# Rotary embedding on one core: units of 4 MiB with 32 KB rows, and a small sine table spread over the partitions by TensorE

## The chip, the cores and the metric

The kernel runs on one core of a Trainium2 chip. The metric is the time of one execution in microseconds (us) as the device reports it. A profile's span is shorter than the time: it goes from the first to the last recorded instruction. In the listings SP, ACT, POOL, DVE and PE are SyncE, ScalarE, GpSimd, VectorE and TensorE, and PEld is TensorE's weight load. A cast load is a load that turns fp32 into fp16 on the way. A DMA "lands" when its end is reported. Slices of the span and units are counted from 0.

## The reference

```python
# x: (8, 8, 1024, 64) float32, freqs: 32, positions: 0..1023, scale 0.5
angles = np.outer(positions * scale, freqs)          # 1024 x 32
cos, sin = np.cos(angles), np.sin(angles)
x_first, x_second = x[..., :32], x[..., 32:]
out_first  = x_first * cos - x_second * sin
out_second = x_first * sin + x_second * cos
```

16.8 MB come in and 16.8 MB go out. The table of sines and cosines is the same for all 64 pairs of batch and head.

## The kernel before

It cuts x into 8 units of 8 heads. (In the cuts of the two kernels here, `...` stands for what is left out; in those of the change the calls of `pin`, which keep an instruction in program order, are left out too.) A unit is 128 partitions x 4096 fp32, so one partition's row is 16 KB of contiguous HBM. Each partition holds 64 positions, and 16 partitions hold a head.

```python
X0f = xin.tile([P, N], FP32, name="X0f")                 # unit 0 in two fp32 halves, from SP and ACT
nc.sync.dma_start(out=X0f[:, : N // 2], in_=xv[0][:, : N // 2])
...                                                      # positions, freqs, second half: ACT's queue
def load(u):                                             # units 1..7: cast to fp16 on the way, POOL's queue
    nc.gpsimd.dma_start(out=X[u].rearrange("p k h j -> p (k h j)"), in_=xv[u])
...                                                      # cfreq = scale/2pi * freqs on all partitions; posf: positions
y = tmp.tile([P, K, half], FP32)                         # 128 x 64 x 32: the whole table, on every partition
nc.vector.tensor_tensor(out=y, in0=posf..., in1=cfreq..., op=ALU.mult)
...                                                      # m, r: range reduction; then sin, ra, cos
for i, u in enumerate((1, 2, 0, *range(3, NU))):
    ps = prods.tile([P, K, 2, half], FP16, tag="ps")     # two buffers
    nc.vector.tensor_tensor(out=ps, in0=X[u], in1=sin_b, op=ALU.mult)
    nc.vector.tensor_tensor(out=X[u], in0=X[u], in1=cos_b, op=ALU.mult)
    nc.vector.tensor_tensor(out=X[u][:, :, 0, :], in0=X[u][:, :, 0, :], in1=ps[:, :, 1, :], op=ALU.subtract)
    nc.vector.tensor_tensor(out=X[u][:, :, 1, :], in0=ps[:, :, 0, :], in1=X[u][:, :, 1, :], op=ALU.add)
    OUT = xout.tile([P, N], FP32, tag="O")
    nc.scalar.copy(out=OUT, in_=X[u]...)                 # back to fp32
    (nc.gpsimd if i < NU // 2 else nc.sync).dma_start(out=ov[u], in_=OUT)
```

## Time and profile before

| What | Before | Where from |
|---|---|---|
| time | 84.59 us median (84.48 to 84.63) | 6 runs |
| span | 82.6 to 83.8 us, median 82.8; the profiled one 83.1 | 44 runs beside the experiments, and the profile |
| VectorE busy | 62.5 us (75%) | the page |
| DMA | full from 2 to 81 us, 405 GB/s of HBM traffic over the span | the page's slices; 33.56 MB / 82.8 us |

The profiled execution of the kernel before was one of the slower ones, by 0.3 us. A comparison of the two profiles alone would be wrong by that much.

### The profile page before, as it was taken

The page shows a single profiled execution, that of the slowest core. Times are in us where ns is not written, and L with a number is a line of the kernel's source. Part 1 is how long each engine was busy: PE and PEld are TensorE (multiplying, and loading weights), DVE is VectorE, ACT ScalarE, POOL GpSimd, SP SyncE. Part 2 cuts the span into 40 slices and gives each one's busy share as a digit, 9 for nine tenths or more (in the row PEclk, how much of TensorE's full clock was granted, in tenths as well). Part 3 has the DMA queues.
Part 4 walks back from the last instruction along what each step waited for, and adds up shares of the span by engine and source line. Part 5 has one row for each costly group of instructions (what it writes and reads, how often), then busy time and mean ns, then how long its engine had stood idle before and what let it go on. Part 6 is the DMA issues. An engine that isn't in the chain of part 4 may idle for free.

```text
span 83.1 us, 154 instructions
## 1 busy us (share of the span) xinstructions
PE 1.1 (1%) x4; PEld 0.9 (1%) x4; DVE 62.5 (75%) x40; ACT 37.4 (45%) x12; POOL 6.7 (8%) x17
## 2 busy tenths in 40 slices
PE   0014000000000000000000000000000000000000
PEld 0013000000000000000000000000000000000000
DVE  0005999699999999999999999999999999000000
ACT  0600005999295098059129408805912950880000
POOL 4970000000002000200200200000000000000000
DMA  2799999999999999999999999999999999999990
GB/s 51 248 363 280 280 272 249 213 225 213 205 217 213 229 209 213 213 209 229 162 379 410 442 418 442 434 434 426 418 457 418 434 442 418 434 418 450 426 426 8
DMA packets 2482, 26.22 MB, mean 316 GB/s; under 512 B 290, under 2 KB 306, under 8 KB 306
## 3 DMA queue, kind: packets, MB, share of 16 engines
q0 software_dynamic: 1584, 15.73, 66.4%
q1 hardware_dynamic: 720, 9.44, 27.4%
q10 hardware_dynamic: 178, 1.06, 3.2%
HBM read 16.79 MB, written 16.78 MB: 404 GB/s over the span
## 4 chain that ended last, share of the span: by engine, by line
DVE 72%; ACT 7%; DMA 6%; DVEq 1%; PE 1%; issue 1%; ACTq 1%
DVE X L137 22%; DVE ps L136 21%; DVE X L138 12%; DVE X L141 10%; DMA freq_row<-in_freqs_dram 6%; ACT OUT L145 4%; DVE r L117 3%; DVE y L108 3%; ACT sinT L121 2%; DVE m L115 1%; DVEq L177 1%; PE cfreq L93 1%; PE pos_ps L101 1%; ACTq L66 0%; DVE posf L105 0%
## 5 line engine op out<-in xcount | busy, mean ns | idle before, releaser
L145 ACT CAST OUT<-X 128x4096 f32<-128x4096 f16 x8 | 28.8, 3605 | 25.0 <-DVE X L141 25.0
L136 DVE TENSOR_TENSOR ps<-X,sinT 128x4096 f16<-128x4096 f16 x8 | 18.3, 2284 | 0.7 <-ACT sinT L121 0.7
L137 DVE TENSOR_TENSOR X<-X,cosT 128x4096 f16<-128x4096 f16 x8 | 18.3, 2292 | 0.3
L138 DVE TENSOR_TENSOR X<-X,ps 128x2048 f16<-128x2048 f16 x8 | 9.8, 1225 | 0.3
L141 DVE TENSOR_TENSOR X<-ps,X 128x2048 f16<-128x2048 f16 x8 | 9.7, 1217 | 0.0
L121 ACT ACTIVATE sinT<-r 128x2048 f16<-128x2048 f32 x1 | 1.9, 1910 | 9.9 <-DVE r L117 9.9
L146 POOL DMA_DIRECT2D out_dram<-OUT x4 | 2.1, 534 | 39.7 <-ACT OUT L145 39.7
L74 POOL DMA_DIRECT2D X<-in_x_dram x7 | 3.9, 569 | 0.8 <-POOLq L163 0.8
L128 ACT CAST X<-X0f 128x4096 f16<-128x4096 f32 x1 | 3.6, 3589 | 0.0
L96 DVE CAST pos_row<-pos_i 16x64 f32<-16x64 int32 x1 | 0.2, 182 | 3.1 <-DMA pos_i<-in_positions_dram 3.1
L105 DVE COPY posf<-pos_ps 128x64 f32<-128x64 f32 x1 | 0.2, 224 | 2.8 <-PE pos_ps L101 2.8
L117 DVE SCALAR_TENSOR_TENSOR r<-m,y 128x2048 f32<-128x2048 f32 x1 | 2.3, 2293 | 0.0
L108 DVE TENSOR_TENSOR y<-posf,cfreq 128x2048 f32<-128x2048 f32 x1 | 2.3, 2286 | 0.0
L121 ACT ACT_TABLE_LOAD x1 | 1.3, 1283 | 2.1 <-issue 2.1
L127 ACT ACTIVATE cosT<-ra,quarter 128x2048 f16<-128x2048 f32 x1 | 2.0, 1987 | 0.0
L115 DVE TENSOR_SCALAR m<-y 128x2048 f32<-128x2048 f32 x1 | 1.2, 1226 | 0.0
L123 DVE TENSOR_SCALAR ra<-r 128x2048 int32<-128x2048 int32 x1 | 1.2, 1226 | 0.0
L89 DVE MEMSET coef<- 1x128 f32 x1 | 0.2, 165 | 0.8 <-PEq L163 0.8
L93 PE MATMUL cfreq<-freq_row,coef 1*128 1x32 f32 x2 | 0.6, 392 | 6.0 <-DMA freq_row<-in_freqs_dram 6.0
L101 PE MATMUL pos_ps<-pos_row,sel 16*128 16x64 f32 x2 | 0.7, 433 | 0.0
L93 PEld LDWEIGHTS cfreq<-freq_row,coef 1*128 1x128 f32 x2 | 0.5, 305 | 6.0 <-issue 6.0
L101 PEld LDWEIGHTS pos_ps<-pos_row,sel 16*128 16x128 f32 x2 | 0.5, 328 | 0.0
(7 smaller groups left out, 1.0 us busy)
## 6 DMA issues: line engine op xcount, KB each, us to landing
out_dram<-OUT POOLq DMA_DIRECT2D x4, 2048.0 KB, 20.5
out_dram<-OUT SPq DMA_DIRECT2D x4, 2048.0 KB, 10.8
X<-in_x_dram POOLq DMA_DIRECT2D x7, 1024.0 KB, 24.4
X0f<-in_x_dram SPq DMA_DIRECT2D x1, 1024.0 KB, 5.2
X0f<-in_x_dram ACTq DMA_DIRECT2D x1, 1024.0 KB, 11.8
pos_i<-in_positions_dram ACTq DMA_DIRECT2D x1, 8.0 KB, 3.4
freq_row<-in_freqs_dram ACTq DMA_DIRECT2D x1, 0.1 KB
```

The lines of the kernel that those rows point to most:

```text
L74: nc.gpsimd.dma_start(out=X[u].rearrange("p k h j -> p (k h j)"), in_=xv[u])
L101: nc.tensor.matmul(out=pos_ps, lhsT=sel.rearrange("q a b -> q (a b)"), rhs=pos_row, start=True, stop=True)
L108: pin(nc.vector.tensor_tensor(out=y, in0=posf.unsqueeze(2).broadcast_to((P, K, half)), in1=cfreq.unsqueeze(1).broadcast_to((P, K, half)), ...
L117: pin(nc.vector.scalar_tensor_tensor(out=r, in0=m, scalar=_MAGIC, in1=y, op0=ALU.subtract, op1=ALU.subtract))
L121: pin(nc.scalar.activation(out=sinT, in_=r, func=AF.Sin, bias=0.0, scale=-_TWO_PI_DN))
L128: pin(nc.scalar.copy(out=X[0].rearrange("p k h j -> p (k h j)"), in_=X0f))
L136: pin(nc.vector.tensor_tensor(out=ps, in0=X[u], in1=sin_b, op=ALU.mult))
L137: pin(nc.vector.tensor_tensor(out=X[u], in0=X[u], in1=cos_b, op=ALU.mult))
L138: pin(nc.vector.tensor_tensor(out=X[u][:, :, 0, :], in0=X[u][:, :, 0, :], in1=ps[:, :, 1, :], op=ALU.subtract))
L141: pin(nc.vector.tensor_tensor(out=X[u][:, :, 1, :], in0=ps[:, :, 0, :], in1=X[u][:, :, 1, :], op=ALU.add))
L145: pin(nc.scalar.copy(out=OUT, in_=X[u].rearrange("p k h j -> p (k h j)")))
L146: (nc.gpsimd if i < NU // 2 else nc.sync).dma_start(out=ov[u], in_=OUT)
```

## The change

Two things. First, units of 16 heads (4 MiB) with 32 KB rows for three of the four cast loads and for the first two stores. This saves row overhead. Second, each position's sine and cosine are computed once, 8 positions a partition. Sixteen matmuls with selection matrices of zeros and ones spread them over the partitions, and sixteen copies bring them out of PSUM, the memory into which TensorE writes. The matrices (`sel`) are made on GpSimd by a memset and a select by index (`affine_select`), called "the select" below. This shortens the start of VectorE.

```diff
-    HEADS = 8
+    HEADS = 16
...
-    pos_i64 = consts.tile([HP, K], positions.dtype)            # 16 rows of 512 B
+    pos_i64 = consts.tile([P, K8], positions.dtype)            # 128 rows of 64 B
...
-    sel = consts.tile([HP, HEADS, HP], FP32)
+    sel = consts.tile([P, G, HEADS, HP], FP16)                 # 128 x 2048
+    nc.gpsimd.dma_start(out=Xf[0][:, :NH], in_=xv[0][:, :NH])  # half of unit 0, cast
     nc.gpsimd.memset(sel, 0.0)
+    nc.gpsimd.dma_start(out=Xf[1], in_=xv[1])
     nc.gpsimd.affine_select(...)
+    for u in range(2, NU):
+        nc.gpsimd.dma_start(out=Xf[u], in_=xv[u])
...
-    y = tmp.tile([P, K, half], FP32)                           # 2048 columns
+    y = tmp.tile([P, K8, half], FP32)                          # 256 columns; m, r, ra, sin, cos too
...
+    for g in range(G):                                         # 16
+        ps = spread.tile([P, 2, K8, half], FP32, tag="g")
+        nc.tensor.matmul(out=ps, lhsT=sel[:, g], rhs=tab, start=True, stop=True)
+        dst = T[:, :, g * K8 : (g + 1) * K8, :]
+        if g % 2 == 0 and g < G // 2:
+            nc.vector.tensor_copy(out=dst, in_=ps)
+        else:
+            nc.scalar.copy(out=dst, in_=ps)
...
+    for u in range(NU):                                        # 4 units, two halves each
+        for s in range(2):
+            pr = tmp.tile([P, KH, 2, half], FP16, tag="pr")    # one buffer
+            ...                                                # the same four operations, then the ACT copy
+            if u >= NU // 2:
+                nc.sync.dma_start(out=ov[u][:, ns], in_=OUT[:, ns])
+        if u < NU // 2:
+            nc.gpsimd.dma_start(out=ov[u], in_=OUT)            # 4 MiB
```

More of the change, by code (lines that the diff above doesn't have):

```diff
@@ L18 @@
 _TWO_PI_DN = float(np.float32(np.uint32(0x40C90FDA).view(np.float32)))
-BUF_O = 4
-BUF_P = 2
 @with_exitstack
@@ L34 @@
     nc = tc.nc
+    pin = tc.keep_in_program_order
     B, Hh, S, D = x.shape
@@ L44 @@
     NU = NBH // HEADS
-    assert S % HP == 0 and D == 2 * half and NBH % HEADS == 0
+    KH = K // 2
+    NH = KH * D
+    K8 = S // P
+    G = P // HP
+    W = K8 * half
+    assert S % HP == 0 and D == 2 * half and NBH % HEADS == 0 and G * K8 == K
     fscale = float(scale)
@@ L54 @@
     psum = ctx.enter_context(tc.tile_pool(name="psum", bufs=1, space=bass.MemoryType.PSUM))
+    spread = ctx.enter_context(tc.tile_pool(name="spread", bufs=6, space=bass.MemoryType.PSUM))
     xin = ctx.enter_context(tc.tile_pool(name="xin", bufs=1))
-    xout = ctx.enter_context(tc.tile_pool(name="xout", bufs=BUF_O))
-    prods = ctx.enter_context(tc.tile_pool(name="prods", bufs=BUF_P))
-    X0f = xin.tile([P, N], FP32, name="X0f")
-    pin = tc.keep_in_program_order
-    nc.sync.dma_start(out=X0f[:, : N // 2], in_=xv[0][:, : N // 2])
-    pos_i64 = consts.tile([HP, K], positions.dtype)
-    pin(nc.scalar.dma_start(out=pos_i64, in_=positions.rearrange("(q k) -> q k", k=K)))
+    xout = ctx.enter_context(tc.tile_pool(name="xout", bufs=3))
+    X0f = xout.tile([P, N], FP32, tag="O")
+    Q = NH // 2
+    pin(nc.sync.dma_start(out=X0f[:, :Q], in_=xv[0][:, NH : NH + Q]))
+    pos_i64 = consts.tile([P, K8], positions.dtype)
+    pin(nc.scalar.dma_start(out=pos_i64, in_=positions.rearrange("(p k) -> p k", k=K8)))
     freq_row = consts.tile([1, half], FP32)
     pin(nc.scalar.dma_start(out=freq_row, in_=freqs[None, :]))
-    pin(nc.scalar.dma_start(out=X0f[:, N // 2 :], in_=xv[0][:, N // 2 :]))
+    pin(nc.scalar.dma_start(out=X0f[:, Q:NH], in_=xv[0][:, NH + Q :]))
     X = [xin.tile([P, K, 2, half], FP16, name=f"X{u}") for u in range(NU)]
-    def load(u):
-        nc.gpsimd.dma_start(out=X[u].rearrange("p k h j -> p (k h j)"), in_=xv[u])
-    sel = consts.tile([HP, HEADS, HP], FP32)
-    load(1)
-    nc.gpsimd.memset(sel, 0.0)
-    nc.gpsimd.affine_select(
+    Xf = [t.rearrange("p k h j -> p (k h j)") for t in X]
+    sel = consts.tile([P, G, HEADS, HP], FP16)
+    pin(nc.gpsimd.dma_start(out=Xf[0][:, :NH], in_=xv[0][:, :NH]))
+    pin(nc.gpsimd.memset(sel, 0.0))
+    pin(nc.gpsimd.dma_start(out=Xf[1], in_=xv[1]))
+    pin(nc.gpsimd.affine_select(
         out=sel, in_=sel, compare_op=ALU.not_equal, fill=1.0, base=0,
-        pattern=[[0, HEADS], [-1, HP]], channel_multiplier=1,
-    )
+        pattern=[[-1, G], [0, HEADS], [-G, HP]], channel_multiplier=1,
+    ))
     for u in range(2, NU):
-        load(u)
+        pin(nc.gpsimd.dma_start(out=Xf[u], in_=xv[u]))
     coef = consts.tile([1, P], FP32)
@@ L93 @@
     nc.tensor.matmul(out=cfreq, lhsT=coef, rhs=freq_row, start=True, stop=True)
-    pos_row = consts.tile([HP, K], FP32)
+    posf = consts.tile([P, K8], FP32)
     pin(nc.vector.tensor_copy(
-        out=pos_row,
-        in_=pos_i64.bitcast(I32).rearrange("p (k t) -> p k t", t=2)[:, :, 0],
-    ))
-    pos_ps = psum.tile([P, K], FP32)
-    nc.tensor.matmul(
-        out=pos_ps, lhsT=sel.rearrange("q a b -> q (a b)"), rhs=pos_row, start=True, stop=True
-    )
-    posf = consts.tile([P, K], FP32)
-    pin(nc.vector.tensor_copy(out=posf, in_=pos_ps))
-    y = tmp.tile([P, K, half], FP32)
+        out=posf, in_=pos_i64.bitcast(I32).rearrange("p (k t) -> p k t", t=2)[:, :, 0]
+    ))
+    y = tmp.tile([P, K8, half], FP32)
     pin(nc.vector.tensor_tensor(
         out=y,
-        in0=posf.unsqueeze(2).broadcast_to((P, K, half)),
-        in1=cfreq.unsqueeze(1).broadcast_to((P, K, half)),
+        in0=posf.unsqueeze(2).broadcast_to((P, K8, half)),
+        in1=cfreq.unsqueeze(1).broadcast_to((P, K8, half)),
         op=ALU.mult,
     ))
-    m = tmp.tile([P, K, half], FP32)
+    m = tmp.tile([P, K8, half], FP32)
     pin(nc.vector.tensor_scalar(out=m, in0=y, scalar1=_MAGIC, scalar2=None, op0=ALU.add))
-    r = tmp.tile([P, K, half], FP32)
+    r = tmp.tile([P, K8, half], FP32)
     pin(nc.vector.scalar_tensor_tensor(
@@ L119 @@
     ))
-    sinT = consts.tile([P, K, half], FP16)
-    pin(nc.scalar.activation(out=sinT, in_=r, func=AF.Sin, bias=0.0, scale=-_TWO_PI_DN))
-    ra = tmp.tile([P, K, half], FP32)
+    tab = consts.tile([P, 2, K8, half], FP16)
+    pin(nc.scalar.activation(out=tab[:, 0], in_=r, func=AF.Sin, bias=0.0, scale=-_TWO_PI_DN))
+    ra = tmp.tile([P, K8, half], FP32)
     pin(nc.vector.tensor_scalar(
@@ L125 @@
     ))
-    cosT = consts.tile([P, K, half], FP16)
-    pin(nc.scalar.activation(out=cosT, in_=ra, func=AF.Sin, bias=quarter, scale=-_TWO_PI_DN))
-    pin(nc.scalar.copy(out=X[0].rearrange("p k h j -> p (k h j)"), in_=X0f))
-    cos_b = cosT.unsqueeze(2).broadcast_to((P, K, 2, half))
-    sin_b = sinT.unsqueeze(2).broadcast_to((P, K, 2, half))
-    for i, u in enumerate((1, 2, 0, *range(3, NU))):
-        ps = prods.tile([P, K, 2, half], FP16, tag="ps")
-        pin(nc.vector.tensor_tensor(out=ps, in0=X[u], in1=sin_b, op=ALU.mult))
-        pin(nc.vector.tensor_tensor(out=X[u], in0=X[u], in1=cos_b, op=ALU.mult))
-        pin(nc.vector.tensor_tensor(
-            out=X[u][:, :, 0, :], in0=X[u][:, :, 0, :], in1=ps[:, :, 1, :], op=ALU.subtract
-        ))
-        pin(nc.vector.tensor_tensor(
-            out=X[u][:, :, 1, :], in0=ps[:, :, 0, :], in1=X[u][:, :, 1, :], op=ALU.add
-        ))
-        OUT = xout.tile([P, N], FP32, tag="O")
-        pin(nc.scalar.copy(out=OUT, in_=X[u].rearrange("p k h j -> p (k h j)")))
-        (nc.gpsimd if i < NU // 2 else nc.sync).dma_start(out=ov[u], in_=OUT)
+    pin(nc.scalar.activation(out=tab[:, 1], in_=ra, func=AF.Sin, bias=quarter, scale=-_TWO_PI_DN))
@@ new lines @@
+    T = consts.tile([P, 2, K, half], FP16)
+    for g in range(G):
+        ps = spread.tile([P, 2, K8, half], FP32, tag="g")
+        nc.tensor.matmul(
+            out=ps.rearrange("p t k j -> p (t k j)"),
+            lhsT=sel[:, g].rearrange("s h q -> s (h q)"),
+            rhs=tab.rearrange("s t k j -> s (t k j)"),
+            start=True, stop=True,
+        )
+        dst = T[:, :, g * K8 : (g + 1) * K8, :]
+        if g % 2 == 0 and g < G // 2:
+            pin(nc.vector.tensor_copy(out=dst, in_=ps))
+        else:
+            pin(nc.scalar.copy(out=dst, in_=ps))
@@ new lines @@
+    pin(nc.scalar.copy(out=Xf[0][:, NH:], in_=X0f[:, :NH]))
+    for u in range(NU):
+        OUT = xout.tile([P, N], FP32, tag="O")
+        for s in range(2):
+            ks = slice(s * KH, (s + 1) * KH)
+            ns = slice(s * NH, (s + 1) * NH)
+            Xs = X[u][:, ks]
+            sin_b = T[:, 0, ks].unsqueeze(2).broadcast_to((P, KH, 2, half))
+            cos_b = T[:, 1, ks].unsqueeze(2).broadcast_to((P, KH, 2, half))
+            pr = tmp.tile([P, KH, 2, half], FP16, tag="pr")
+            pin(nc.vector.tensor_tensor(out=pr, in0=Xs, in1=sin_b, op=ALU.mult))
+            pin(nc.vector.tensor_tensor(out=Xs, in0=Xs, in1=cos_b, op=ALU.mult))
+            pin(nc.vector.tensor_tensor(
+                out=Xs[:, :, 0, :], in0=Xs[:, :, 0, :], in1=pr[:, :, 1, :], op=ALU.subtract
+            ))
+            pin(nc.vector.tensor_tensor(
+                out=Xs[:, :, 1, :], in0=pr[:, :, 0, :], in1=Xs[:, :, 1, :], op=ALU.add
+            ))
+            pin(nc.scalar.copy(out=OUT[:, ns], in_=Xf[u][:, ns]))
+            if u >= NU // 2:
+                pin(nc.sync.dma_start(out=ov[u][:, ns], in_=OUT[:, ns]))
+        if u < NU // 2:
+            pin(nc.gpsimd.dma_start(out=ov[u], in_=OUT))
```

## The prediction

> **What bounds the kernel now.** I began with the slices of the page, because a kernel that only streams 16.8 MB in and 16.8 MB out should first be asked whether its DMA engines ever rest.
>
> ```profile
> DVE  0005999699999999999999999999999999000000
> ACT  0600005999295098059129408805912950880000
> ...
> DMA  2799999999999999999999999999999999999990
> GB/s 51 248 363 280 280 272 249 213 225 213 205 217 213 229 209 213 213 209 229 162 379 410 442 418 442 434 434 426 418 457 418 434 442 418 434 418 450 426 426 8
> ```
>
> One slice is 83.1/40 = 2.08 us. The DMA row is full from slice 2 to slice 38; VectorE starts in slice 3 and ends in slice 33. The GB/s row halves in the load phase only because a load that casts fp32 to fp16 is counted by the bytes that it writes: 213 written is 426 read from HBM. So the rate is nearly flat.
>
> The chain that ended last says something else, and I don't follow it to the end:
>
> ```profile
> DVE 72%; ACT 7%; DMA 6%; DVEq 1%; PE 1%; issue 1%; ACTq 1%
> ```
>
> It goes back through VectorE because its last compute piece is the ACT cast that starts at 70.86 us and takes 3.60. That ends at 74.46; the span ends at 83.1. One 2 MiB store cannot explain 8.6 us if the queues are empty, so I looked at the stores' landings and at the DMA by window:
>
> ```profile
> L146 SPq DMA_DIRECT2D out_dram<-OUT x4: 332/332/343, 53.7 to 74.5; - x4
> ...
> DMA to landing us min/median/max: 7.7/16.1/21.9
> ```
>
> ```profile
> 0.00:4.00 4.00, 0.00 (x0) 0.00 (x0) 0.17 (x2) 1.28 (x1) 2.86 (x10) 1.00 0.52 147
> 4.00:8.00 4.00, 1.08 (x4) 0.92 (x4) 1.01 (x3) 0.00 (x0) 1.68 (x4) 1.00 1.05 324
> 18.00:36.00 18.00, 0.00 (x0) 0.00 (x0) 17.83 (x11) 9.81 (x3) 1.07 (x2) 1.00 1.04 217
> ...
> 46.00:78.00 32.00, 0.00 (x0) 0.00 (x0) 24.54 (x15) 15.15 (x5) 0.53 (x1) 1.00 1.01 432
> ```
>
> The last two columns are the DMA share and GB/s. In 18 to 36 us the engines read 2 x 217 = 434 GB/s, in 46 to 78 us they write 432. The quickest store landed 7.7 us after its issue, though 2.1 MB at 432 GB/s is 4.9 us: each store stands in a line. The kernel is bound by DMA from about 2 us to about 82 us. VectorE and ScalarE come second, but not by much: if the queues were empty, the last store, issued at 74.5, would need some 1.3 us to start (my allowance; SP's first load is issued at 0.75 us and the DMA row stirs just short of 2) and 4.9 to move, ending at 80.7. The compute side has about 1 us of slack.
>
> **What the Trainium skill says.** "DMA: Bandwidth & Descriptors", section "Where 436 GB/s comes from", gives 16 x 32 B x 850 MHz = 435.2 GB/s as the ceiling of the SBUF ports. The trace agrees: 432 and 434 are within 1% of it. The same page, "Queues, rings and completion order", says that an engine takes turns between queues packet by packet, and "Issuing engines are not separate DMA queues" says that using several issuing engines saves only issue time. The trace agrees as far as it shows it: SP's and POOL's stores together move 432 GB/s in 46 to 78 us, no more than one direction did before. "TensorE: Matmul & The Clock Gate", section "Wait — 56ns, not 53.3ns?", gives 426.7 ns between matmuls of 512 columns in a cold array, 215.7 warm; the trace of before has no such matmul.
>
> **The change, part by part.**
>
> *Longer rows.* Before, 14 of the 16 MiB of loads go in cast loads of 2 MiB, with rows of 16 KB in HBM, and all 16 MiB of stores too. After, 12 MiB of cast loads (3 units) and 8 MiB of stores (2 units) have rows of 32 KB: 20 of 32 MiB. The rest stays: 2 MiB fp32 loads with 8 KB rows, one 2 MiB cast load, four half-unit stores. The number of bytes is the same. What can a longer row save? Only the cost per row. From the window 46 to 78:
>
> ```profile
> DMA packets 955, 13.81 MB, mean 432 GB/s; under 512 B 112, under 2 KB 112, under 8 KB 112
> ...
> q1 hardware_dynamic: 481, 7.09, 51.8%
> q0 software_dynamic: 474, 6.72, 49.0%
> ```
>
> The shares sum to 100.8% of 16 engines: 516 us of packet time for 843 rows of 16 KB (13.81 MB / 16384), 612 ns each. At the skill's 435.2 GB/s (27.2 B/ns an engine) a row takes 602 ns. So some 10 ns a row are overhead, and the 100.8% says that rows overlap a little and hide part of it. By rate the total loss is (435.2 - 432)/435.2, 0.7% of the 77.7 us that 33.55 MB take at 432 GB/s, or 0.57 us. Half of that goes away on 20 of 32 MiB: 0.57 x 0.5 x 0.63 = 0.18 us. Even if the overhead per row were twice what I read, it would be under 0.4 us.
>
> *Positions as 128 rows of 64 B instead of 16 of 512 B.* Eight small packets an engine in place of one. I put them at 25 to 30 ns each (an estimate from nothing but the overhead of a row above and a little for the access), so up to 0.2 us of DMA time, at the worst moment, the start. It also delays the positions and the frequencies behind them in the same queue: they may land up to 2 us later than now (now freqs' landing at 5.9 us starts the table).
>
> *The table built small.* y, r (2.29 us each), m and ra (1.23) on 2048 columns become four operations on 256. Taking (2286 - 224)/(2048 - 64) = 1.04 ns per column from y and posf gives about 0.16 + 256 x 1.04 = 0.43 us for y and r, and 0.3 for m. sin and cos (1.91, 1.99) become about 0.4 and 0.5. Removed from the path: pos_ps and posf (0.7), and 9.7 - 2.0 = about 7 us from positions to cos. Added: 16 matmuls 128x512 with a weight load each, at 0.45 us, cold; 12 casts on ACT, at 192 + 512 x 0.833 = 0.62 us each (fixed part and slope from the 3605 ns cast of 4096 columns and the 1910 ns sine of 2048), and 4 on VectorE at 0.16 + 512 x 1.04 = 0.7. The first half of the table (8 tiles) paces at TensorE's 0.45: 3.6 us plus the last copy, 0.7. With freqs landed at 6 to 7.5 us the small table is done at 8.6 to 10, the first half of the spread at 13 to 14.5. VectorE now starts at 15.24. It needs the first half of unit 0 too, which shares the engines with the two fp32 loads (4 MiB together), and lands about where unit 1 lands now, 13.4 us (12.1 after its issue at 1.3). So VectorE starts at 13.5 to 14.5, 1 to 2 us earlier.
>
> *The eight half-units.* Same operations and shapes: 2.29 + 2.29 + 1.22 + 1.22, 6.92 us from one to the next as now, so VectorE ends at about 69 to 70 and the last ACT cast at 72.5 to 74. ACT must finish 12 copies (until about 16.5) and the cast of unit 0's second half (3.6) before the second half-unit at 20.4: just in time, a wait of up to 1 us possible. All this only gives the compute side slack of 2 to 3 us instead of 1. On the path that sets the end it is worth nothing.
>
> *Supply of stores.* Loads end at about 42 us, as now (slice 19 to 20). Unit 0 is stored whole at about 31 us, unit 1 at 45, then halves at 52, 59, 66 and 73. At 432 GB/s from 42 us the engines have written 8.6 MB at 62 us (ready by then: 12.6) and 13.2 at 72.5 (ready 14.7): no gap. Units twice as large in the POOL stores do not starve the queue because loads cover the first 42 us.
>
> Sum: -0.2 (rows) + 0.1 (small packets), -0.1 us: 84.5 becomes 84.4.
>
> **Rivals.** (1) *The table was on the path, and the time falls by its 1 to 2 us or more*: for it, the chain, 72% VectorE; against it, DMA rows full to slice 38 and landings of 7.7 us and more. It would give 82.5 to 83.5. (2) *The row overhead is larger than it looks, above all for casts*: the window 18 to 36 has a share of 104%, rows of about 627 ns. If those 25 ns over 602 all vanished by half on the 20 MiB, 80 rows of 16 KB an engine would save 80 x 12 = 1.0 us: 83.5. Against it: the rate there is 434, so the rows overlap. (3) *The compute side takes over*: GpSimd has to fill and select 128x2048 instead of 16x128 (select now 0.33 us), the positions come late, the copies are slow. VectorE would have to start later than about 16.5 us to show; then 85 to 86. (4) *A gap at the start*, unit 1's load behind the larger memset: 4 MiB are queued before it, about 9.8 us of work, so no.
>
> **Range and chances.** Both states are DMA-bound with the same bytes at 99% of the ceiling, so little can move. The 80% range is 83.6 to 85.1, its low end from rival 2, its high end from a worse start. Faster by over 2% needs 82.8: 5%. Slower by over 2% needs 86.2: 3%.
>
> **What would show it.** DMA full from slice 2 to 38 again, 430 to 434 GB/s in both phases, half as many packets in q0; ACT's last cast ending 1 to 2 us earlier, the last store's landing time longer by as much. I am wrong if the rate in a phase moves by over 1%, if the DMA row has a hole, or if the first full slice of DMA shifts.

## The result

The changed kernel takes 84.88 us (84.82 to 85.06, 6 runs) against 84.59 of before. The ratio is 1.0041, interval 1.0028 to 1.0055. That is above noise a little slower. Executions over 1.5% slower than the fastest of the same kernel are left out of the means. A ratio is the mean time of one kernel's fast runs over that of the other's fast runs of the same rounds, so it is not quite the ratio of the medians.

The slices of the changed kernel's page, to be laid beside those of before:

```profile
DVE  0029657999899999999999999999999999400000
ACT  0600337999993098059219607903940880492000
...
DMA  3899997997998899799989989998999999999991
GB/s 51 327 319 269 301 341 170 254 254 151 230 254 190 190 254 238 158 238 254 127 349 412 507 364 428 475 460 357 420 436 412 428 444 412 452 420 436 436 412 55
...
q0 software_dynamic: 864, 15.73, 66.3%
```

DMA again stays full from slice 2 to slice 38. Both rows jump more, but this is only the grain of the view: a row of 32 KB is booked whole in the slice where it starts. With each record spread over its time, the engines are busy for 98% or more of each slice from 1 to 38. Queue q0 moves the same 15.73 MB in 864 packets instead of 1584. Slice 1 has 327 GB/s against 248: the start is better. (This row counts cast loads by what they write; a count by what is read from HBM, under e5 and e9, has 1.50 MB against 1.35 by 6 us.)

The windows and the landings, as before (the last two columns are DMA share and GB/s):

```profile
0.00:4.00 4.00, 0.00 (x0) 0.00 (x0) 0.17 (x2) 1.28 (x1) 2.95 (x7) 1.00 0.56 181
...
18.00:36.00 18.00, 0.00 (x0) 0.00 (x0) 17.40 (x11) 11.09 (x5) 0.54 (x1) 0.57 1.02 218
36.00:44.00 8.00, 0.00 (x0) 0.00 (x0) 7.86 (x6) 4.44 (x2) 0.00 (x0) 0.50 1.04 262
46.00:78.00 32.00, 0.00 (x0) 0.00 (x0) 24.98 (x15) 15.19 (x5) 0.53 (x1) 0.50 1.00 430
```

```profile
DMA to landing us min/median/max: 6.8/12.3/19.7
```

Steady rates are those of before within the grain of the view. The quickest store lands 6.8 us after its issue instead of 7.7. So the last store waits less, which means the compute side is nearer to being the bound, not further from it. The groups and the order of time say why:

```profile
L98 DVE CAST posf<-pos_i 128x8 f32<-128x8 int32 x1 | 2.5, 2496 | 4.7 <-DMA pos_i<-in_positions_dram 4.7
L82 POOL TENSOR_SCALAR_AFFINE_SELECT sel<-sel 128x2048 f16<-128x2048 f16 x1 | 3.9, 3865 | 0.1
```

```profile
4.29 3.87 POOL L82 TENSOR_SCALAR_AFFINE_SELECT sel<-sel 128x2048 f16<-128x2048 f16 x1
5.69 2.50 DVE L98 CAST posf<-pos_i 128x8 f32<-128x8 int32 x1 [4.69 <-DMA pos_i<-in_positions_dram]
...
14.61 2.29 DVE L149 TENSOR_TENSOR pr<-X,T 128x4096 f16<-128x4096 f16 x1 [0.31 <-ACT T L136]
...
22.02 2.29 DVE L149 TENSOR_TENSOR pr<-X,T 128x4096 f16<-128x4096 f16 x1 [0.40 <-ACT X L137]
...
27.82 1.22 DVE L154 TENSOR_TENSOR X<-pr,X 128x2048 f16<-128x2048 f16 x1
29.07 2.29 DVE L149 TENSOR_TENSOR pr<-X,T 128x4096 f16<-128x4096 f16 x1
...
71.35 3.60 ACT L157 CAST OUT<-X 128x4096 f32<-128x4096 f16 x1 [3.40 <-DVE X L154]
```

The lines of the kernel before with which these are compared:

```profile
4.15 0.18 DVE L96 CAST pos_row<-pos_i 16x64 f32<-16x64 int32 x1 [3.15 <-DMA pos_i<-in_positions_dram]
...
15.24 2.29 DVE L136 TENSOR_TENSOR ps<-X,sinT 128x4096 f16<-128x4096 f16 x1 [0.72 <-ACT sinT L121]
...
28.03 1.22 DVE L141 TENSOR_TENSOR X<-ps,X 128x2048 f16<-128x2048 f16 x1
29.17 2.28 DVE L136 TENSOR_TENSOR ps<-X,sinT 128x4096 f16<-128x4096 f16 x1
...
70.86 3.60 ACT L145 CAST OUT<-X 128x4096 f32<-128x4096 f16 x1 [3.32 <-DVE X L141]
```

The cast of 8 numbers a partition takes 2.5 us instead of 0.2, and ends where GpSimd's select ends (8.16). VectorE's first product starts at 14.61, only 0.6 us earlier than before, and VectorE then loses 0.4 us waiting for the second half of unit 0. Every half-unit takes 7.05 us instead of 6.92. The next product starts when the addition ends (27.82 + 1.22, then 29.07), because both use the one product buffer; before, with two, it started 0.1 us sooner. (In e2, which has the spread table and two buffers, it starts sooner too, at 20.34 against an addition that ends at 20.43, and the interval is 6.93.) The last cast ends at 74.95, half a microsecond later than before.

Where did the time go? It did not go into the span. The spans of the changed kernel's runs are 82.6 to 82.9 us, those of before have the median 82.8. Time minus span, run by run, is 2.14 to 2.22 us here and 1.73 to 1.82 before. The span is equal or 0.1 us better; 0.4 us come after it or ahead of it.

### The profile page after: what moved, and what is told of

The parts are those of the page before. It is cut to its first block, busy times and chain, and to the rows that moved or that the text cites. A ratio compares the mean times of both kernels' runs of the same rounds, so it can differ in the third digit from the quotient of the medians.

```text
span 82.7 us, 185 instructions
## 1 busy us (share of the span) xinstructions
PE 6.0 (7%) x18; PEld 2.5 (3%) x18; DVE 62.4 (75%) x43; ACT 40.6 (49%) x24; POOL 9.1 (11%) x12
## 3 DMA queue, kind: packets, MB, share of 16 engines
q0 software_dynamic: 864, 15.73, 66.3%
## 4 chain that ended last, share of the span: by engine, by line
DVE 58%; ACT 15%; DMA 6%; issue 5%; PE 4%; DVEq 1%; ACTq 0%
DVE pr L149 19%; DVE X L150 19%; DVE X L154 9%; DVE X L151 6%; DMA pos_i<-in_positions_dram 6%; ACT T L136 5%; ACT OUT L157 4%; PE ps L126 4%; ACT X L137 4%; DVE posf L98 3%; DVEq L192 1%; DVE r L111 1%; DVE y L102 1%; ACT tab L120 1%; ACT tab L115 1%
## 5 line engine op out<-in xcount | busy, mean ns | idle before, releaser
L149 DVE TENSOR_TENSOR pr<-X,T 128x4096 f16<-128x4096 f16 x8 | 18.3, 2292 | 0.9 <-ACT X L137 0.4
L150 DVE TENSOR_TENSOR X<-X,T 128x4096 f16<-128x4096 f16 x8 | 18.3, 2292 | 0.3
L151 DVE TENSOR_TENSOR X<-X,pr 128x2048 f16<-128x2048 f16 x8 | 9.8, 1224 | 0.3
L154 DVE TENSOR_TENSOR X<-pr,X 128x2048 f16<-128x2048 f16 x8 | 9.7, 1218 | 0.0
L136 ACT CAST T<-ps 128x512 f16<-128x512 f32 x12 | 6.3, 621 | 1.9 <-PE ps L126 1.9
L98 DVE CAST posf<-pos_i 128x8 f32<-128x8 int32 x1 | 2.5, 2496 | 4.7 <-DMA pos_i<-in_positions_dram 4.7
L126 PE MATMUL ps<-tab,sel 128*128 128x512 f16 x16 | 5.4, 500 | 4.1 <-ACT tab L120 4.0
L134 DVE CAST T<-ps 128x512 f16<-128x512 f32 x4 | 2.8, 691 | 1.7 <-PE ps L126 1.7
L82 POOL TENSOR_SCALAR_AFFINE_SELECT sel<-sel 128x2048 f16<-128x2048 f16 x1 | 3.9, 3865 | 0.1
L126 PEld LDWEIGHTS <-sel 128*128 128x128 f16 x16 | 2.0, 122 | 6.9 <-issue 4.3
```

The costliest lines, as they stand in the source:

```text
L82: pin(nc.gpsimd.affine_select(out=sel, in_=sel, compare_op=ALU.not_equal, fill=1.0, base=0, pattern=[[-1, G], [0, HEADS], [-G, HP]], chann ...
L98: pin(nc.vector.tensor_copy(out=posf, in_=pos_i64.bitcast(I32).rearrange("p (k t) -> p k t", t=2)[:, :, 0]))
L126: nc.tensor.matmul(out=ps.rearrange("p t k j -> p (t k j)"), lhsT=sel[:, g].rearrange("s h q -> s (h q)"), rhs=tab.rearrange("s t k j -> s ...
L134: pin(nc.vector.tensor_copy(out=dst, in_=ps))
L136: pin(nc.scalar.copy(out=dst, in_=ps))
L149: pin(nc.vector.tensor_tensor(out=pr, in0=Xs, in1=sin_b, op=ALU.mult))
```

## The experiments

All twelve had five rounds, each beside runs of the kernel before (84.58 to 84.75 us medians).

**e1, long rows undone.** The changed kernel with each 4 MiB DMA in two halves:

```diff
-        pin(nc.gpsimd.dma_start(out=Xf[u], in_=xv[u]))
+        for c in range(2):
+            pin(nc.gpsimd.dma_start(out=Xf[u][:, c * NH : (c + 1) * NH], in_=xv[u][:, c * NH : (c + 1) * NH]))
```

(The first load of 4 MiB and the two stores are cut in the same way.)

> The changed kernel with every 4 MiB load and store cut into two DMAs of half a row (16 KB), issued at the same places; all else the same. Theory: longer rows save only row overhead, 0.2 us, and the rise of the time by 0.3 us comes from elsewhere, from something outside the profiled span (the span of the changed kernel is 82.7 against 83.1 before, yet its time is 84.88 against 84.59). Then the span here is 82.8 to 83.0 and the time 85.0 to 85.2, 1.005 to 1.008 of before. Rival A: the long rows cost time (a 32 KB row is slower to finish or to report); then the time falls to 84.5 and the ratio to 1.00.

Measured: 84.76 us, ratio 1.0011 (0.999 to 1.0031), spans 82.7 to 83.0, time minus span 1.90 to 1.97. The span is that of the changed kernel within 0.1 us, so long rows are worth nothing that shows. The time missed both expectations, because time minus span, which I had taken as fixed, fell by 0.25 us.

**e2, the table part alone.** The kernel before with the small table, 8 spreading matmuls and 8 copies.

> The kernel before, its 2 MiB units and 16 KB rows kept, with the small table spread by TensorE (8 matmuls) in place of the full table. Theory: the start of VectorE by a microsecond or two is worth nothing, as DMA sets the end; span within 0.3 us of 83.1. If the cost outside the span belongs to the table part (TensorE's instructions, more of them to fetch, more semaphores), the time minus the span is here 2.0 to 2.2 us instead of 1.8 and the time 84.7 to 84.9. Rival: if the table was on the path, the time falls by 1 us or more, to 83.5. If the cost outside belongs to the long units, the time is 84.5.

Measured: 84.61 us, ratio 0.9996, spans 82.6 to 83.3, time minus span 1.76 to 1.82. VectorE is now ready early, and waits for its first unit:

```profile
L147 DVE TENSOR_TENSOR ps<-X,T 128x4096 f16<-128x4096 f16 x8 | 18.3, 2285 | 2.7 <-DMA X<-in_x_dram 2.7
```

Its first product starts at 13.41 instead of 15.24, its last cast ends at 73.56 instead of 74.46, and the time does not move. The last cast gained less than the first product because it had to wait for DMA: its output buffer was still being stored.

```profile
69.96 3.60 ACT L156 CAST OUT<-X 128x4096 f32<-128x4096 f16 x1 [4.32 <-DMA out_dram<-OUT]
```

The table was not on the path, and it brings no cost outside the span here.

**e3, no spread.** The changed kernel with `T` filled by a memset, without the 16 matmuls and 16 copies. Its output is wrong, which doesn't matter for the time.

> The changed kernel with the 16 matmuls and 16 copies of the spread taken out and the large table filled by one memset: a wrong result on purpose. If the cost outside the span comes from the added TensorE instructions, time minus span goes back from 2.2 to 1.8 us and the time to about 84.4, ratio 0.998. If it comes from the DMA part of the change, nothing changes: 84.9, ratio 1.004. If VectorE's start mattered, which is earlier still here, the time would fall by 1 us or more.

Measured: 84.52 us, ratio 0.9989, spans 82.6 to 83.0, time minus span 1.73 to 1.83. The excess outside the span is gone.

**e4, unused matmuls.** The kernel before with 16 matmuls of 128x512 on zeros, their outputs read by nobody.

> The kernel before with 16 unused matmuls of 128x512 and their weight loads added on TensorE, nothing else. If TensorE's instructions alone lengthen the time outside the span, the time rises by 0.3 to 0.4 us, to 84.9 (ratio 1.004), with the span unchanged at 83.1. If not, 84.55 and ratio 1.000.

Measured: 87.69 to 89.88 us (half of the runs count as slow by their distance from the fastest); ratio of the fast ones 1.0442. It is a miss, and a useful one. The scheduler put all 16 in front of the matmul for the positions, which starts at 13.14 instead of 6.44, so VectorE's first product started 6.5 us later (21.72).

```profile
13.14 0.43 PE L106 MATMUL pos_ps<-pos_row,sel 16*128 16x64 f32 x2
```

This profile is of the slowest run (89.88 us), and no other run of e4 has one. Time minus span stayed at 1.76 to 1.81, so the bare TensorE instructions are not what lengthens it. The span of the profiled run is 5.3 us above the usual 82.8, less than the 6.5: the compute side had slack, and it can be measured. (The fast runs grew by 3.1 to 4.3 us; how late VectorE was in them is not known.)

**e6 and e7, the compute side late.** Two VectorE operations of 2.3 us before the first product, in the kernel before (e6) and in the changed one (e7, on a tile of its own):

```diff
+    for _ in range(2):
+        pin(nc.vector.tensor_tensor(out=m, in0=y, in1=y, op=ALU.mult))
```

> The kernel before with two more VectorE operations of 2.3 us each in front of the first product: the compute side starts 3.9 us later. Theory (DMA sets the end, the compute side has 1 to 2 us of slack): the time rises by 2.0 to 2.9 us, to 86.6 to 87.5. Rival (the compute side is the bound): it rises by the whole 3.9, to 88.5. If DMA had plenty of slack to give, it rises by under 1.

> The changed kernel with the same two operations in front of its first product, which start right after VectorE's last copy of the table: 4.3 us later. Its last cast ends at 74.95, half a microsecond later than before (74.46), and its DMA no later, so its slack should be smaller, 0.5 to 1.2 us: the time rises by 3.1 to 3.8, to 88.0 to 88.7. Rival (the prediction's step: the change gives the compute side more slack, 2 to 3 us): it rises by 1.3 to 2.3.

Measured: e6 86.99 us, ratio 1.0277; e7 87.88, ratio 1.0390. e6 is in its range. e7 rose by 3.0 over the changed kernel's 84.88, on the small-slack side but 0.1 short of its range; its time minus span is 1.88 to 1.98, and its span rose by 3.3 (82.7 to 86.0). The DMA row of e6's page now has holes at its end, which it had in neither kernel:

```profile
DMA  3899999999999999999999999999999998990982
```

The last casts of the two, e6 first:

```profile
74.16 3.60 ACT OUT L147
```

```profile
75.17 3.60 ACT OUT L161
```

From these two the slack can be worked out. In both, the span ends 7.2 us after the end of the last cast (77.76 to 84.9 and 78.77 to 86.0). The last store finds the queue empty: by the DMA records the one before it has moved its last row at 76.8 and 77.7, about 1 us before the last is issued. Before, the last cast ends at 74.46, so the compute side alone would end at 81.6 to 81.7, 1.1 us ahead of the usual span of 82.8. In e6's profiled run the frequencies happened to land 0.4 us earlier than in that of before (their matmul starts at 5.59 against 6.02); with so early a landing the slack before would be 1.6. After the change the compute side would end at 82.1 to 82.2, 0.6 us ahead of 82.7. So the change took half of the slack or more, by one profile of each kernel.

**e5 and e9, short rows at the switch.** By the traces' DMA records, the kernels with long rows are ahead at 38 us and have lost most of it at 43, when the loads end and the stores begin. In the table, each packet's bytes are spread evenly over its time, and cast loads are counted by what they read from HBM. "Lost" is 5 us minus the MB moved from 38 to 43 us at 431 GB/s.

```
                       MB by 6 us  by 38 us  by 43 us  by 70 us   lost in 38-43
before                    1.35      15.10     17.03     28.68        0.5 us
e2  (short rows)          1.40      15.15     17.03     28.67        0.6
e1  (short rows)          1.46      15.21     17.12     28.77        0.6
changed kernel            1.50      15.31     17.08     28.76        0.9
e3  (long rows)           1.46      15.27     17.08     28.76        0.8
e5  (last load short)     1.51      15.30     17.03     28.71        1.0
e9  (stores short)        1.47      15.28     17.05     28.70        0.9
```

e5 cuts the last load into 16 KB rows, e9 the two large stores, with the diff of e1 at those lines only.

> The changed kernel with the last load alone (unit 3, 4 MiB) cut into two DMAs of 16 KB rows. In the trace of the changed kernel the rates in both steady phases are a little higher (433 and 432 against 431 GB/s), yet loads end at the same time as before: the last rows of the loads, just ahead of the first store, take about 2.1 us instead of 1.23; before, rows of 16 KB there take up to 1.15 instead of 0.63. Theory: that loss at the switch from loads to stores grows with the row, and gives back what the long rows save; then loads end 0.3 to 0.5 us earlier here and the span is 82.3 to 82.5, the time 0.3 us under the changed kernel's 84.88. Rival: the loss is a fixed time of about 0.5 us or more that does not follow the row; then the span is 82.7 and the time 84.8 or more.

> The changed kernel with its 32 KB loads, but the two 4 MiB stores cut into DMAs of 16 KB rows. Cutting the last load instead (e5) did not help: by the traces the long-row kernels are 0.4 to 0.5 us ahead at 38 us and have lost most of it at 43 us. Theory: that extra loss comes from the long rows of the first store meeting the last loads. Then the loads keep what they gained, and the span is 82.3 to 82.5, 0.3 us under the changed kernel's 82.8 (time 84.5 if time minus span stays at 2.16). Rival: the loss follows the long rows of either side, or none of them; then span 82.7 to 82.9, time 84.8 to 85.0.

Measured: e5 85.03 us, ratio 1.0062, span 82.8 to 83.2. e9 85.04, ratio 1.0032 (0.9996 to 1.0069), span 82.7 to 83.0. Both theories fell: neither the last load's rows nor the stores' rows alone make the extra loss. It stands in all kernels that have long rows on one side or both, and is smaller in e1 and e2, which have none. The records show where it lies. The DMA engines don't rest there; the last rows of the loads, just ahead of the first store's rows at about 42 us, take longer: a 32 KB row up to 2.3 us instead of 1.23, a 16 KB row up to 1.3 instead of 0.62. Summed over the rows that take a quarter or more longer than at 432 GB/s, this makes 0.4 to 0.6 us an engine in the table's kernels with short rows, 0.8 to 1.0 in those with long ones, and nothing in e12 below: about what the table calls lost. In e5, whose last load has short rows, more of them are stretched (35 against 20 to 26 in before, e1 and e2). Why is open.

The table shows something else too: the lead of 0.1 MB (0.25 us) over before at 6 us is in e1 as well, so it doesn't belong to the rows. It goes with the new start, of which the order of the first loads is the likely part; no run tests that order alone.

**e8, the positions' cast on ScalarE.**

```diff
-    pin(nc.vector.tensor_copy(
+    pin(nc.scalar.copy(
         out=posf, in_=pos_i64...
```

> The changed kernel with the cast of the positions on ScalarE instead of VectorE: on VectorE it takes 2.5 us instead of 0.2 while GpSimd's select of 128x2048 runs, and ends when the select ends. Theory: the select holds VectorE's cast up; on ScalarE it takes 0.2 us, and VectorE's first product starts 1 to 2 us earlier (at 12.5 to 13.5 instead of 14.6, if unit 0 has landed). The time does not fall for it: within 0.15 us of the changed kernel's (84.7 to 85.0), as DMA sets the end. Rival: the table is on the path in the changed kernel; then the time falls by 1 us or more. Time minus span, 2.16 us in the changed kernel and 1.78 before, may change with the build; if it is 1.8 here, the excess does not belong to any of the change's work.

Measured: 84.77 us, ratio 1.0025 (1.0013 to 1.0037), spans 82.7 to 82.8, time minus span 2.02 to 2.08. VectorE's first product starts at 13.91 and the last cast ends at 74.24, both 0.7 us earlier; the time stays. The expected 1 to 2 us were too much: another VectorE operation, the next but one, ran into the same select.

```profile
4.28 3.87 POOL L82 TENSOR_SCALAR_AFFINE_SELECT sel<-sel 128x2048 f16<-128x2048 f16 x1
```

```profile
6.84 1.46 DVE L109 TENSOR_SCALAR m<-y 128x256 f32<-128x256 f32 x1
```

It takes 0.29 us in the changed kernel, where it runs after the select, and ended at 8.30 here, just after the select (8.15). The Trainium skill, "SBUF — State Buffer", section "Who interferes with whom", says that copies, casts and tensor_scalar in a 2-port mode share a port pair with GpSimd, and that the second to come is blocked until the first is done. The trace agrees: 2.50 us for the cast in the changed kernel, 1.46 for the tensor_scalar here (it doesn't show the mode in which they ran). In e2, whose select is over at 4.99, the same cast takes 0.17 at 6.14.

**e11, matmuls without copies.** The changed kernel with the 16 matmuls, and the table by a memset. Its output is wrong, which doesn't matter for the time.

> The changed kernel with its 16 spreading matmuls but without the 16 copies (table by a memset, a wrong result on purpose). It splits the excess outside the span, which is gone when both are taken out (e3: 1.78 us) and 2.16 in the changed kernel. If it belongs to TensorE's part, time minus span is 2.1 to 2.2 and the time 84.9; if to the copies, 1.8 and 84.5; in between, the excess follows the build and no one part.

Measured: 84.45 us, ratio 0.9964 (0.9928 to 1.0000), spans 82.6 to 82.8, time minus span 1.75 to 1.84. The excess goes with the copies, or with the matmuls' waits for them, not with the matmuls.

**e10, the version that these point to.** e8, e9's stores, and 8 copies of 1024 columns instead of 16 of 512:

```diff
-        ps = spread.tile([P, 2, K8, half], FP32, tag="g")
+        ps = spread.tile([P, 2, 2, W], FP32, tag="g")     # two matmuls fill it, one copy empties it
```

> The version that the experiments point to: short rows in the two large stores, the positions cast on ScalarE, the table copied out of PSUM in 8 pieces of 1024 columns instead of 16 of 512. Theory: the compute side ends at 74.0 or earlier; span 82.3 to 82.5; time minus span nearer to 1.8 with fewer instructions. Time 84.2 to 84.6, ratio 0.996 to 1.000 of before. If the switch loss stays and the excess too, 84.8.

Measured: 84.56 us, ratio 0.9979 (0.9938 to 1.0019), spans 82.6 to 83.1, time minus span 1.74 to 1.83. The excess is gone with half the copies, and the time is 0.3 us under that of the changed kernel. The span did not fall, as the loss at the switch stayed (0.9 us), so it does not beat the kernel before beyond noise.

**e12, no switch.** The kernel before with all stores from SP:

```diff
-        (nc.gpsimd if i < NU // 2 else nc.sync).dma_start(out=ov[u], in_=OUT)
+        nc.sync.dma_start(out=ov[u], in_=OUT)
```

> The kernel before with all eight stores issued by SP. The first three are issued at 26, 33 and 40 us, and then no longer stand behind the loads in POOL's queue but take turns with them: there is no sharp switch from loads to stores at 42 us. In all runs so far between 38 and 43 us some 0.5 us of DMA time is lost with short rows and 0.9 us with long ones. Theory: the loss belongs to the switch; without it the span falls by 0.3 to 0.5 us, to 82.3 to 82.5, and the time to 84.1 to 84.3 (ratio 0.995). Rival: turning between reads and writes row by row costs more than one switch; then the span rises, to 83.2 or more.

Measured: 85.14 us, ratio 1.0055 (1.0027 to 1.0083), spans 83.2 to 83.7. The rival holds. From 38 to 43 us nothing is lost now (2.14 MB moved), but from 18 to 38, in which the first stores enter, the engines move 414 GB/s instead of 431. One sharp switch was cheaper here than taking turns.

## Why the prediction was right or wrong

The time lies in the range, for the reason given: DMA sets the end. The direction was not right: the time rose by 0.3 us where the sum said -0.1.

- **What bounds the kernel: right.** A later compute side raises the time by less than the delay (e6), an earlier one does nothing (e2, e8). The slack that I had put at "about 1 us" from an allowance is 1.1 to 1.6 us by e6.
- **Longer rows, -0.2 us: right in mechanism, and given back.** The steady rates rose as the step said, by the DMA records from 431 to 433 GB/s between 18 and 38 us. That is 0.2 us over the loads. The step missed that the switch from loads to stores costs 0.8 to 1.1 us with long rows instead of 0.5 to 0.6. With long rows undone (e1) the span is the same.
- **Positions in small rows, +0.1 us: mis-sized.** The step put a small packet at 25 to 30 ns; the DMA records have 11 ns. The Trainium skill, "DMA: Bandwidth & Descriptors", section "Measured (HBM→SBUF, 128 partitions, SWDGE, issued from GpSimd)", reckons about 10.5 ns a packet for a load of 4 KB in 64 packets. That is near, but the page doesn't say there how many engines share the 64, and the positions come from ACT's queue, so the agreement may be chance. The positions landed 4.9 us after their issue instead of 3.4, the frequencies no later (their matmul starts at 5.86 us, against 6.02 before).
- **The small table and the spread: sizes right, the sum wrong.** y took 0.42, m 0.29, sin 0.42, cos 0.51, a copy 0.62 on ACT and 0.69 on VectorE, all within 0.1 us of the step. (The two durations that it names for the ACT copy would give 0.64 us rather than 0.62; nothing hangs on it.) The matmuls came 0.43 us apart, as cold ones do by the section cited. But "the last ACT cast at 72.5 to 74" failed: it ended at 74.95. Missing were the cast held up by the select (2.3 us; the rivals asked only whether GpSimd itself would be late), the wait for unit 0's second half (0.4 us, within what the step allowed), and 0.1 us a half-unit from the single product buffer, which "6.92 us from one to the next as now" overlooked. So "slack of 2 to 3 us instead of 1" was wrong in sign: it fell to 0.6.
- **The sum, -0.1 us: the span did this** (82.7 against 82.8), in part by luck. The rows' gain was given back, and a better start, which the sum did not have (0.25 us at 6 us, in e1 too), stands in its place; 0.1 us is also no more than the runs scatter. The time rose by 0.3 because of a term that the prediction did not have: 0.4 us outside the span. It is there in the six kernels with 16 copies out of PSUM (1.88 to 2.23 us: the changed kernel, e1, e5, e7, e8, e9), and not in those with 8 or none (1.72 to 1.84: before, e2, e3, e4, e6, e10, e11, e12). Its size differs among the six: e1, e7 and e8 have 0.1 to 0.3 us less of it than the changed kernel, with the same copies. The number of instructions alone is not it: e4 has 188 on its page and no excess, the changed kernel 185. The cause is not shown beyond this: it takes the sixteen copies, and which of their work makes it, or whether something that goes with them does, stays open.
- **Rivals.** Rival 1 is refuted by e2; rival 2 by e1. Rival 3 did not come, but was 0.6 us away. Rival 4, a gap at the start, did not come.
- **The signs.** DMA full to slice 38 and the steady rates came as said, and none of the three signs of being wrong did. But two signs that should have come did not: the last cast ended 0.5 us later and not 1 to 2 us earlier, and the landing of the last store, the quickest in both, got shorter (6.8 against 7.7 us) and not longer. Both belong to the part on the compute side, which was wrong.

## What to carry to other kernels

When the DMA row is full, ask of each part of a change whether it moves bytes, rates or the turns between loads and stores; here the rest was worth nothing. A chain of waits that runs through a compute engine is no proof of a bound: delay that engine on purpose, and the part of the delay that does not come out as time is the slack. And compare spans with times, since a change can lengthen what no profile of the span shows.

## What the Trainium skill lacked or had wrong

- "DMA: Bandwidth & Descriptors" compares no rows of different length for loads with a cast or for stores on trn2; its table goes by the size of a transfer. Here 16 KB rows moved 431 GB/s and 32 KB rows 433 in cast loads (18 to 38 us), below its ceiling of 435.2.
- The same page has nothing on the change from loads to stores on one core: 0.5 to 0.6 us lost in most kernels with 16 KB rows, 0.8 to 1.1 us with 32 KB rows on either side, in the last rows of the loads. Nor does it say what turns between the two cost: 414 GB/s instead of 431 over the 20 us in which they began (e12), and 0.5 us more in all.
- "GPSIMD Engine Reference" names no time for a select by index: 3.87 us for 128x2048 fp16, and 1.82 for a memset of the same tile.
- "Runtime: NRT & Kernel Launch" doesn't say that the time around a kernel may depend on the kernel's own compute instructions: time minus span was 1.72 to 1.84 us in eight kernels and 1.88 to 2.23 in the six with 16 copies out of PSUM.
